# Attention with a bias on one core: the second half of pair 0's q is loaded after the bias's first half, and the four bias exps move one score slot back

## The chip, the core and the metric

The kernel runs on one core of a Trainium2 chip. The metric is the device time of one execution in microseconds. TensorE (PE), VectorE (DVE), ScalarE (ACT) and GpSimd (POOL) are engines that each take their own instructions in order; SyncE (SP) only issues DMAs here, and ScalarE and GpSimd issue some too.

## The reference

Four batches of eight heads, 1024 queries and 1024 keys of 64 numbers, one bias matrix shared by all heads:

```python
scale = 1.0 / np.sqrt(head_dim)
scores = scale * np.matmul(q, k.transpose(0, 1, 3, 2))
scores = scores + bias                       # bias: (1, 1, 1024, 1024)
scores_max = np.max(scores, axis=-1, keepdims=True)
attn = np.exp(scores - scores_max) / (np.sum(np.exp(scores - scores_max), axis=-1, keepdims=True) + 1e-8)
return np.matmul(attn, v).astype(np.float32)
```

## The kernel before

**The arithmetic.** The kernel uses exp(scale * s + b) = exp(scale * s) * exp(b) and subtracts no maximum. Scores are made transposed, keys on the partitions and queries along the row, so that the exps can go straight into the second matmul as its stationary operand. v carries a 65th column of ones, whose result is the row sum; a reciprocal and a multiply at the end divide by it.

**Pairs, banks and slots.** Two heads form a pair (`pr` 0 to 15), because two heads of 64 numbers fill the 128 partitions of one transpose. A *bank* is one score matmul: a head h of the pair, a query half qh (512 queries) and a key chunk kc (128 keys). There are 512 banks; in a pair the order is query half, key chunk, head, so that banks 0 to 15 are query half 0 of pair 0, banks 16 to 31 query half 1, and pair 1 starts at bank 32. Banks are gathered in *slots*: slot 0 is bank 0, slot 1 banks 1 and 2, and from slot 2 on each slot is three banks, `[3, 4, 5]`, `[6, 7, 8]` and so on. So slot 6 is banks 15, 16 and 17, the first that needs query half 1. A slot is one PSUM tile (`ps_s`, two buffers), filled by `s_fill` with three matmuls (line 130) and emptied by `s_exp` with one ScalarE instruction of 1536 elements (line 137), which writes the exps into the ring E (six tiles of 12 banks).

**The bias.** It is loaded in two halves of 1 MB (as bf16) into `btraw`. A *bias slot* `("B", qh, k0)` takes one of the two `ps_s` buffers: `b_fill` makes 16 transposes (line 145), and `b_exp` one ScalarE instruction of 2048 elements (line 150), which leaves exp(bias) for four key chunks of one query half in `eb`. There are four of them: (0, 0), (0, 4), (1, 0), (1, 4). VectorE multiplies E by `eb` (`mul_pair`, lines 156, 159, 162), which can start only when the first bias slot is through. The last two banks of the kernel, 510 and 511, get their bias on TensorE instead (`late_bias`, line 133).

**q and k.** Each pair's q and k are loaded as they are and transposed on TensorE in four pieces (`transpose_pe`, line 89): k or q, first or second half. A copy on VectorE takes a piece out of PSUM: for k line 102, for q line 98, which also multiplies by a mask so that each head's q has zeros where the other head's is. Pair 0 is loaded in parts: the first halves on SP's and ScalarE's queues (lines 244 to 247), the second half of k, the second half of q and the first half of the bias on GpSimd's queue, in this order:

```python
nc.gpsimd.dma_start(out=kr0[:, :, QC:, :]..., in_=kf[0][:, :, QC * D:])      # 261
nc.gpsimd.dma_start(out=qr0[:, :, QC:, :]..., in_=qf[0][:, :, QC * D:])      # 262
nc.gpsimd.dma_start(out=btraw[:, :QC, :], in_=bf_[:, :QC, :])                # 263
```

Behind them on this queue come v of pair 0, the bias's second half, and q, k and v of the next pairs (lines 317 to 321).

**The value matmuls.** `av_bank` adds one bank's share to the output of its unit (pair, head, query half) with four matmuls (line 187), in one of two PSUM buffers (`xa`, `xb`) that the transposed pieces use as well. When a unit's eight banks are in, VectorE divides (lines 197 and 199) and SP stores. The last unit is done by `av_last` in two halves of its queries (line 223), so that both can be finished side by side; its reciprocals are line 232.

**The order.** Slots 0 to 2 and the parts around them are written out by hand (lines 244 to 321). From slot 3 on a planner (lines 325 to 610) plays the three engines with given costs and due times and writes the instructions down in the order in which it starts them. ScalarE's order is fixed in the list `order`: the score slots in turn with the bias slots inserted. Before the change it begins S3, S4, S5, S6, B(0,0), S7, B(0,4), S8, S9, B(1,0), S10, B(1,4), S11. The due times `raw_at[0]` (the landing of pair 0's k and q second halves) and `bias_at` (the landing of the two bias halves) are in ns of the planner's clock; they cost no instruction, but decide where a step is put in TensorE's order. Since every engine works in order, a step that waits holds what is put behind it.

Of the kernel before, what the change touches and what calls it, by code (L numbers as in the profile page):

```python
# [15 lines left out]
def kernel(  # L16
# [15 lines left out]
    nc = tc.nc  # L32
# [7 lines left out]
    QC = NCH // 2  # L40
# [5 lines left out]
    bf_ = bias.rearrange("a b (p c) k -> p (a b c) k", p=P)  # L46
# [12 lines left out]
    btraw = consts.tile([P, NCH, S], BF)  # L59
# [47 lines left out]
    NB = len(banks)  # L107
# [106 lines left out]
    def av_last(x, bs, tag):  # L214
        first = len(last_left[x]) == 8
        if first:
            po[x] = (ps_x if tag != "s" else ps_s).tile([P, M, D1], F32, tag=tag, name="po")
        acc = po[x]
        for b in bs:
            last_left[x].remove(b)  # L220
        for i in range(M):
            for b in bs:
                nc.tensor.matmul(acc[:, i, :], e_at(b, 1)[:, 0, (x * M + i) * P:(x * M + i + 1) * P],
                                 vall[:, 2 * NP - 1, banks[b][3], :], start=first and i == 0 and b == bs[0],
                                 stop=not last_left[x] and b == bs[-1], skip_group_check=True)
        if last_left[x]:
            return None

        def evac():
            oh = small.tile([P, M, D], F32, name=f"oh{x}")  # L230
            rs = small.tile([P, M, 1], F32, name=f"rh{x}")
            nc.vector.reciprocal(rs[:], acc[:, :, D:D1])
            q = (nc.scalar, nc.sync)[x]
            if x == 0:
                for i in range(M):
                    nc.scalar.activation(oh[:, i, :], acc[:, i, :D], ACTF.Copy, scale=rs[:, i, :])
            else:
                nc.vector.tensor_tensor(oh[:], acc[:, :, :D], rs[:].to_broadcast([P, M, D]), op=ALU.mult)
            q.dma_start(out=of[2 * NP - 1][:, QC + x * M:QC + (x + 1) * M, :], in_=oh[:])
        return evac  # L240

    with tc.manual_schedule():
# [16 lines left out]
        nc.gpsimd.memset(qT0[D:, 0, :HQ], 0.0)  # L259
        nc.gpsimd.memset(qT0[:D, 1, :HQ], 0.0)  # L260
        nc.gpsimd.dma_start(out=kr0[:, :, QC:, :].rearrange("p t c d -> p t (c d)"), in_=kf[0][:, :, QC * D:])  # L261
        nc.gpsimd.dma_start(out=qr0[:, :, QC:, :].rearrange("p t c d -> p t (c d)"), in_=qf[0][:, :, QC * D:])
        nc.gpsimd.dma_start(out=btraw[:, :QC, :], in_=bf_[:, :QC, :])
        for x in range(2):
            for y in range(2):
                nc.vector.memset(mask[x * D:(x + 1) * D, y, :], 1.0 if x == y else 0.0)
# [59 lines left out]
        EXP, EXP0, QK, AV, TP = 427, 62, 216, 170, 350  # L326
        MUL, COPYQ, COPYK, EVAC, SEM = 600, 650, 420, 620, 80
        order = [("S", g) for g in range(3, NS)]
        for at, x in ((4, (0, 0)), (6, (0, 4)), (9, (1, 0)), (11, (1, 4))):
            order.insert(at, ("B",) + x)  # L330
        NO = len(order)
        T0 = 8000.0
# [2 lines left out]
        act_end = []  # L335
        x_free = {"xa": T0 - 500, "xb": T0 + 100}
        x_unit = {}
        bias_at = [13300, 20800]
        raw_at = {0: (5900, 7800), 1: (22200, 23500), 2: (26000, 28500)}
        pieces = [(0, 0, 1)]  # L340
        for pr in range(1, NP):
            pieces += [(pr, 1, 0), (pr, 0, 0), (pr, 1, 1), (pr, 0, 1)]
# [109 lines left out]
        def pe_last():  # L452

            best = None
            for x in range(2):
                left = last_left[x]
                if not left or (x == 1 and last_tag[0] is None):
                    continue
                steps = [[b] for b in left if b not in (NB - 4, NB - 3)] or [[NB - 4, NB - 3]]
                for bs in steps:  # L460
                    if any(b not in mul_at for b in bs):
                        continue
                    ready = max(mul_at[b] for b in bs) + SEM
                    tag = last_tag[x]
                    if tag is None and x == 0:
                        free, tag = min((x_free[y], y) for y in x_free)
                        ready = max(ready, free + SEM)
                    elif tag is None:
                        if len(act_end) < NO - 1 or len(filled) < NO:
                            continue  # L470
                        tag = "s"
                        ready = max(ready, act_end[NO - 2] + SEM)
                    c = (max(ready, t_pe), x, bs, tag)
                    if best is None or c[0] < best[0]:
                        best = c
            if best is None:
                return None
            ready, x, bs, tag = best
            cost = len(bs) * AV // 2

            def emit(t):
                if last_tag[x] is None and x == 0:
                    x_free[tag] = 1e12
                last_tag[x] = tag
                evac = av_last(x, bs, tag)
                if evac:
                    dve_q.append((t + cost + SEM, 1, EVAC, lambda t2: evac()))
            return ready, cost, emit

        def pe_av():  # L490
            if av_next >= NA:
                return pe_last()
            b = av_order[av_next]
            if b not in mul_at:
                return None
            ready = mul_at[b] + SEM
            u = unit_of(b)
            if banks[b][3] == 0:
                free, tag = min((x_free[x], x) for x in x_free)
                ready = max(ready, free + SEM)  # L500
            else:
                tag = x_unit[u]

            def emit(t):
                nonlocal av_next
                x_unit[u] = tag
                x_free[tag] = 1e12
                evac = av_bank(b, tag)
                av_next += 1
                if evac:  # L510
                    def run(t2):
                        evac()
                        x_free[tag] = t2 + EVAC
                    dve_q.append((t + AV + SEM, 3 if u == (NP - 1, 0, 1) else 1, EVAC, run))
            return ready, AV, emit
# [125 lines left out]
```

## Time and profile before

| | us |
|---|---|
| median of 7 runs | 250.39 (249.88 to 251.39) |
| the profiled execution | 250.58 |
| its span in the profile | 248.8 |
| ScalarE busy | 240.0 (96%) |
| TensorE busy | 229.3 (92%) |
| VectorE busy | 220.6 (89%) |
| first bias half: issue to landing | 9.4 |
| second bias half: issue to landing | 10.7 |

The span runs from the first to the last instruction of one execution; the time around it belongs to the execution too. Times in the timelines are us from the start of the span. A timeline line gives start, length, engine, line of the kernel, operation, what is written and read, the number of instructions merged into it, and in brackets how long the engine was idle before it and what ended that. The granted TensorE clock is 0.997 of full speed in the mean.

### The profile page before, as it was taken

To read this page: it belongs to the slowest core of one execution; us is meant where nothing else is said; L and a number is where in the kernel's file an instruction comes from. 1 tells how busy PE (TensorE), PEld (TensorE's weight loads), DVE (VectorE), ACT (ScalarE), POOL (GpSimd) and SP (SyncE) were. 2 spreads that over 40 slices of the span, in tenths; PEclk is the share of its full clock that TensorE was granted. 3 is DMA by queue.
4 is the path that set the end of the run, shared out by engine and by line. 5 is a ranking of instruction groups with operands and counts; after the bars stand their busy time and mean duration, and the time that the engine had idled before them with its cause. 6 is when DMAs were issued, how large, how long until landed. Compare 5 with 4: busy or idle time off the path is not lost.

```text
span 248.8 us, 7212 instructions
## 1 busy us (share of the span) xinstructions
PE 229.3 (92%) x3160; PEld 140.9 (57%) x3160; DVE 220.6 (89%) x393; ACT 240.0 (96%) x183; POOL 53.7 (22%) x74
## 2 busy tenths in 40 slices
PE   8768999999999999999999999999999999998991
PEld 4246656666555565655655665555565556565561
DVE  5236999999999999999999989999999999998882
ACT  5999999999999999999999999999999999999991
POOL 6653544104013050315050400501600000000000
PEclk9999999999999999999999999999999999999998
DMA  5999999924935659495868921592991101020211
GB/s 116 186 203 188 199 134 201 91 87 55 158 47 92 79 92 123 89 127 86 129 85 115 131 54 44 77 139 42 150 67 42 45 35 53 3 84 3 87 41 47
DMA packets 48464, 23.80 MB, mean 96 GB/s; under 512 B 34480, under 2 KB 44592, under 8 KB 48176
## 3 DMA queue, kind: packets, MB, share of 16 engines
q0 software_dynamic: 42272, 14.42, 53.5%
q1 hardware_dynamic: 5872, 8.72, 9.8%
q8 instruction: 25, 0.41, 0.7%
q10 hardware_dynamic: 288, 0.20, 0.2%
q14 instruction: 7, 0.06, 0.1%
HBM read 29.36 MB, written 8.39 MB: 152 GB/s over the span
## 4 chain that ended last, share of the span: by engine, by line
ACT 62%; PE 15%; DVE 14%; DMA 4%; issue 2%; POOL 1%; ACTq 0%; POOLq 0%
ACT E L137 59%; PE ps L130 10%; DVE E L162 5%; DMA btraw<-in_bias_dram 4%; PE po L187 3%; ACT eb L150 3%; DVE qT L98 2%; DVE E L159 2%; DVE oall L199 2%; PE px L89 1%; DVE E L156 1%; DVE rs L197 1%; DVE kT L102 1%; PE pb L145 0%; POOL kr L261 0%
## 5 line engine op out<-in xcount | busy, mean ns | idle before, releaser
L137 ACT ACTIVATE E<-ps 128x1536 bf16<-128x1536 f32 (+2 forms) x172 | 230.0, 1700 | 0.4 <-PE ps L130 0.4
L130 PE MATMUL ps<-qT,kT 128*128 128x512 bf16 x512 | 138.4, 378 | 8.2 <-ACT E L137 5.3
L187 PEld LDWEIGHTS <-E 128*128 128x128 bf16 x2016 | 81.4, 98 | 40.1 <-DVE E L162 5.2
L187 PE MATMUL po<-vall,E 128*128 128x65 bf16 x2016 | 92.6, 194 | 2.5 <-DVE E L162 1.3
L159 DVE TENSOR_TENSOR E<-E,eb 128x2048 bf16<-128x2048 bf16 x66 | 79.8, 1217 | 6.9 <-ACT eb L150 6.5
L162 DVE TENSOR_TENSOR E<-E,eb 128x1024 bf16<-128x1024 bf16 x116 | 76.7, 684 | 2.7 <-ACT E L137 1.9
L130 PEld LDWEIGHTS <-kT 128*128 128x128 bf16 x512 | 45.1, 96 | 39.5 <-issue 8.4
L75 POOL DMA_DIRECT2D kr<-in_k_dram x15 | 10.5, 701 | 90.4 <-PE px L89 84.5
L81 POOL DMA_DIRECT2D vall<-in_v_dram x32 | 28.2, 885 | 4.6 <-DVE kT L315 3.6
L199 DVE TENSOR_TENSOR oall<-po,rs 128x256 f32<-128x256 f32 x63 | 26.7, 425 | 2.2
L98 DVE TENSOR_TENSOR qT<-px,mask 128x1024 bf16<-128x1024 bf16 x31 | 21.3, 688 | 3.9 <-PE px L89 3.1
L76 POOL DMA_DIRECT2D qr<-in_q_dram x15 | 10.8, 718 | 30.0 <-PE px L89 25.5
L102 DVE COPY kT<-px 128x512 bf16<-128x512 bf16 x30 | 12.6, 421 | 1.8 <-PE px L89 1.2
L197 DVE RECIPROCAL rs<-po 128x4 f32<-128x4 f32 x63 | 11.2, 177 | 2.0 <-PE po L187 1.7
L89 PEld LDWEIGHTS <-qr 128*64 128x64 bf16 x248 | 8.0, 109 | 8.6 <-issue 5.9
L89 PE MATMUL px<-ident,qr 128*64 128x128 bf16 x248 | 12.8, 225 | 0.0
L89 PE MATMUL px<-ident,kr 128*64 128x128 bf16 x240 | 12.4, 224 | 0.1
L89 PEld LDWEIGHTS <-kr 128*64 128x64 bf16 x240 | 7.7, 109 | 7.8 <-issue 3.6
L150 ACT ACTIVATE eb<-pb 128x2048 bf16<-128x2048 bf16 x4 | 7.5, 1879 | 0.4 <-PE pb L145 0.4
L145 PE MATMUL pb<-ident,btraw 128*128 128x128 bf16 x64 | 4.7, 226 | 2.5 <-ACT eb L150 1.5
L145 PEld LDWEIGHTS <-btraw 128*128 128x128 bf16 x64 | 4.4, 147 | 3.3 <-issue 1.6
L156 DVE TENSOR_TENSOR E<-E,eb 128x1024 bf16<-128x1024 bf16 (+2 forms) x7 | 4.6, 686 | 0.2 <-ACT E L137 0.2
(44 smaller groups left out, 27.2 us busy)
## 6 DMA issues: line engine op xcount, KB each, us to landing
out_dram<-oall SPq DMA_DIRECT2D x28, 256.0 KB, 2.0
vall<-in_v_dram POOLq DMA_DIRECT2D x32, 128.0 KB, 6.2
kr<-in_k_dram POOLq DMA_DIRECT2D x15, 256.0 KB, 4.2
qr<-in_q_dram POOLq DMA_DIRECT2D x15, 256.0 KB, 5.8
btraw<-in_bias_dram POOLq DMA_DIRECT2D x2, 1024.0 KB, 10.0
out_dram<-oall SPq DMA_DIRECT2D x7, 128.0 KB, 3.8
k0f<-in_k_dram SPq DMA_DIRECT2D x2, 128.0 KB, 3.0
q0f<-in_q_dram ACTq DMA_DIRECT2D x1, 128.0 KB, 2.7
```

The source lines that it names most:

```text
L81: nc.gpsimd.dma_start(out=vall[:, 2 * pr + t, :, :D], in_=vf[pr, :, t])
L89: nc.tensor.transpose(px[t * D:(t + 1) * D, c, :], src[:, t, half * QC + c, :], ident[:])
L98: nc.vector.tensor_tensor(dst[:, :, half * HQ:(half + 1) * HQ], px.rearrange("p c q -> p (c q)").unsqueeze(1).to_broadcast([P, 2, HQ]), ma ...
L102: nc.vector.tensor_copy(dst[:, half * QC:(half + 1) * QC, :], px[:])
L130: nc.tensor.matmul(ps[:, j, :], kT[:, kc, :], qT[:, h, qh * HQ:(qh + 1) * HQ], start=True, stop=b not in late_bias)
L137: nc.scalar.activation(e_at(slots[g][0], n), open_ps.pop(("S", g))[:, :n, :], ACTF.Exp, scale=scale)
L150: nc.scalar.activation(eb[:, qh, k0:k0 + 4, :], open_ps.pop(("B", qh, k0))[:, :4, :], ACTF.Exp)
L159: nc.vector.tensor_tensor(e, e, eb[:, qh, kc:kc + 2, :].unsqueeze(2).to_broadcast([P, 2, 2, HQ]), op=ALU.mult)
L162: nc.vector.tensor_tensor(e, e, eb[:, qh, kc:kc + 1, :].to_broadcast([P, n, HQ]), op=ALU.mult)
L187: nc.tensor.matmul(acc[:, i, :], e[:, 0, i * P:(i + 1) * P], vall[:, 2 * pr + h, kc, :], start=(kc == 0 and i == 0), stop=(kc == NCH - 1), ...
L197: nc.vector.reciprocal(rs[:], acc[:, :, D:D1])
L199: nc.vector.tensor_tensor(oall[:, c0:c0 + QC, :], acc[:, :, :D], rs[:].to_broadcast([P, QC, D]), op=ALU.mult)
```

## The change

Three things. On GpSimd's queue the load of the second half of pair 0's q is issued after the load of the bias's first half instead of before it. The four bias slots are inserted one place later in `order`, which then begins S3, S4, S5, S6, S7, B(0,0), S8, B(0,4), S9, S10, B(1,0), S11, B(1,4), S12; the planner's due times for the landings are set to match. And in the plan of the last unit, banks 508 and 509 (`NB - 4`, `NB - 3`) are steps of their own, each as soon as it is multiplied, instead of one step of two banks behind all others.

```diff
@@ -259,8 +259,8 @@
         nc.gpsimd.dma_start(out=kr0[:, :, QC:, :].rearrange("p t c d -> p t (c d)"), in_=kf[0][:, :, QC * D:])
+        nc.gpsimd.dma_start(out=btraw[:, :QC, :], in_=bf_[:, :QC, :])
         nc.gpsimd.dma_start(out=qr0[:, :, QC:, :].rearrange("p t c d -> p t (c d)"), in_=qf[0][:, :, QC * D:])
-        nc.gpsimd.dma_start(out=btraw[:, :QC, :], in_=bf_[:, :QC, :])
@@ -326,7 +326,7 @@
         order = [("S", g) for g in range(3, NS)]
-        for at, x in ((4, (0, 0)), (6, (0, 4)), (9, (1, 0)), (11, (1, 4))):
+        for at, x in ((5, (0, 0)), (7, (0, 4)), (10, (1, 0)), (12, (1, 4))):
             order.insert(at, ("B",) + x)
@@ -335,8 +335,8 @@
-        bias_at = [13300, 20800]
-        raw_at = {0: (5900, 7800), 1: (22200, 23500), 2: (26000, 28500)}
+        bias_at = [12900, 20200]
+        raw_at = {0: (5900, 13700), 1: (22200, 23500), 2: (26000, 28500)}
@@ -456,7 +456,7 @@
-                steps = [[b] for b in left if b not in (NB - 4, NB - 3)] or [[NB - 4, NB - 3]]
+                steps = [[b] for b in left]
                 for bs in steps:
```

## The prediction

> **What bounds the kernel now.** I read the page's busy times first, then ScalarE's timeline, then the chain of waits, then TensorE's and VectorE's timelines around the four bias slots, and last the DMA landings and GpSimd's issues. The busy times say that ScalarE (ACT) is the long engine:
>
> ```profile
> PE 229.3 (92%) x3160; PEld 140.9 (57%) x3160; DVE 220.6 (89%) x393; ACT 240.0 (96%) x183; POOL 53.7 (22%) x74
> ```
>
> ScalarE's timeline (start, length, line, count, and in brackets the idle time before) says where the missing 4% is:
>
> ```profile
> 5.60 1.57 ACT L137 ACTIVATE E<-ps 128x512 bf16<-128x512 f32 x2 [0.18 <-PE ps L130]
> 7.38 6.82 ACT L137 ACTIVATE E<-ps 128x1536 bf16<-128x1536 f32 x5 [0.20 <-PE ps L130]
> 14.62 1.88 ACT L150 ACTIVATE eb<-pb 128x2048 bf16<-128x2048 bf16 x1 [0.42 <-PE pb L145]
> 16.39 1.44 ACT L137 ACTIVATE E<-ps 128x1536 bf16<-128x1536 f32 x1
> ...
> 27.15 215.97 ACT L137 ACTIVATE E<-ps 128x1536 bf16<-128x1536 f32 x161
> ```
>
> From 7.38 us to 243.12 us ScalarE has one wait, 0.42 us before the first bias exp. After it the exps follow each other at 215.97 / 161 = 1.341 us. An exp without a wait begins about 0.11 us before its predecessor's listed end (16.39 against 14.62 + 1.88 = 16.50), so that wait costs 0.42 + 0.11 = 0.53 us. Everything after 14.62 is a gapless run of fixed length: whatever delays ScalarE before it moves the end by as much, and a later engine can't give it back.
>
> Who holds ScalarE at 14.62 is told by the chain of waits and by the first landings:
>
> ```profile
> 3.26 0.71 POOL qr L262
> 3.97 9.36 DMA btraw<-in_bias_dram
> 13.33 0.05 issue
> 13.37 1.22 PE pb L145 x16
> 14.62 1.88 ACT eb L150
> ```
>
> ```profile
> kr<-in_k_dram POOLq DMA_DIRECT2D x1, 128.0 KB, 3.5
> qr<-in_q_dram POOLq DMA_DIRECT2D x1, 128.0 KB, 5.0
> ```
>
> GpSimd issues k's second half at 2.43, q's at 3.26 and the bias at 3.97; they land at 2.43 + 3.5 = 5.9, 3.26 + 5.0 = 8.3 and 3.97 + 9.36 = 13.33. On TensorE and VectorE, the same stretch:
>
> ```profile
> 8.14 0.39 PE L130 MATMUL ps<-qT,kT 128*128 128x512 bf16 x1 [0.33 <-DVE kT L315]
> 8.88 0.81 PE L130 MATMUL ps<-qT,kT 128*128 128x512 bf16 x3 [0.35 <-ACT E L137]
> 9.62 0.41 PE L89 MATMUL px<-ident,qr 128*64 128x128 bf16 x8
> 10.22 0.81 PE L130 MATMUL ps<-qT,kT 128*128 128x512 bf16 x3 [0.19 <-ACT E L137]
> 11.56 0.81 PE L130 MATMUL ps<-qT,kT 128*128 128x512 bf16 x3 [0.54 <-ACT E L137]
> ```
>
> ```profile
> 10.07 0.69 DVE L98 TENSOR_TENSOR qT<-px,mask 128x1024 bf16<-128x1024 bf16 x1 [1.99 <-PE px L89]
> 16.53 2.36 DVE L159 TENSOR_TENSOR E<-E,eb 128x2048 bf16<-128x2048 bf16 x2 [5.76 <-ACT eb L150]
> ```
>
> The second half of q is transposed at 9.62, copied at 10.07, and first used at 11.56: that is score slot 6, banks 15, 16 and 17, of which 16 and 17 are query half 1. Its exp is the last of the five at 7.38, ends at 14.20 and began near 14.20 - 1.44 = 12.76.
>
> **Moved: the q load behind the bias.** GpSimd's two issues swap; their sum (0.72 + 0.58 = 1.30 us) and what follows in that queue are unchanged, and SP's and ACT's queues are not passed. The three landings came in the order of issue, and all three are issued by 4.56 in either order, so I take the queue as served in order: the same bytes end at the same time, only the last arrival is now q's. Hence q's second half lands at 13.33 instead of 8.3. Low end: some engines run dry of the bias early; at 1024 KB in 13.33 - 8.26 = 5.07 us, q's 128 KB are 0.63 us, so 12.7. High end: v's first pieces, issued from 8.13 on, share the engines, and GpSimd's wait for one of them ends only at 14.75: 14.7. The diff's own due time is 13.7. I take 13.33, the row of the same bytes.
>
> From there the chain to ScalarE is, in this trace's durations: start of the transposes 0.04 (13.33 to 13.37 for the bias), eight transposes 0.41, hand-over 0.04, VectorE's masked copy 0.69, hand-over 0.05 (8.14 after kT's copy), the two matmuls of banks 16 and 17: (0.81 - 0.38) / 2 + 0.38 = 0.59, hand-over 0.04. Bank 15 doesn't need it; the row at 8.14 shows one bank waiting alone for its half while the others were already filled. Sum 1.86, so slot 6's exp begins at 15.19 instead of 12.76: **2.43 us later**. This lies wholly on the path: slots 3 to 5 are the only exps whose data is there, they end near 12.86, and ScalarE takes its instructions in order, so slot 7 and the bias exp stand behind the wait.
>
> **Moved: the four bias slots.** The bias's first half now lands before 13.33, its transposes need the score buffer that slot 6's exp frees near 16.63, take 1.21 us, and lie under slot 7's 1.34. The 0.53 us wait is thus gone: **-0.53 us**. Cover of the other three is the same single score exp (1.34 against 1.13 to 1.21 plus 0.09 of hand-overs), the second bias half is used 3 us later than now; taken at nothing, with 0.1 us each if a queued value matmul stands in front, so 0 to 0.4 in all. Slot 11, which needs pair 1, is filled near 25.6, about as now (25.84), from transposes that now start at 22.29 and 23.64: nothing.
>
> VectorE's first multiply goes from 16.53 to the first bias exp's new end: slot 6 from 15.19 to 16.64, slot 7 to 17.98, bias to 19.75, so 3.2 us later, where ScalarE is 1.9 later. The extra 1.3 us of backlog must fit into idle time. The stretches from 27.15 to 243 show VectorE idle for 9.8 us in sum (0.6 to 1.3 in each 25), so it is absorbed; if it isn't, up to 1.3 us come at the end. I take 0. The E ring holds 72 banks; 21 instead of 18 wait at its fullest start.
>
> **Changed: the last value steps.** Banks 508 and 509 become single steps instead of a pair. The number of matmuls is the same. Four of them, 0.92 / 20 = 0.05 us each, can run before bank 509's multiply. What stands behind is VectorE, busy with the other unit's division until 243.81 and at the last reciprocals from 243.75:
>
> ```profile
> 242.98 0.92 PE L223 MATMUL po<-vall,E 128*128 128x65 bf16 x20 [0.19 <-DVE E L156]
> ```
>
> So -0.2 to +0.2, taken 0. The due times at lines 338 and 339 cost no instruction; they make the plan put q's transposes after slot 5's fill instead of after slot 4's.
>
> **Sum.** 2.43 - 0.53 = +1.90 us. The profiled execution took 250.58 (span 248.8 and 1.8 around it), so 252.48; the median of the seven runs is 0.19 lower: **252.3**.
>
> **Rival 1, TensorE loses its clock too.** Slot 5's fill ends at 11.03; with slot 6 blocked TensorE idles until 13.37, 2.34 us. The longest idle time after the start is now 1.32 us, and the granted clock stays 1.00. If the clock fell, the rate is that of the first dummies, 12 of 256 columns in 2.74 us, 0.11 us for 128 columns: eight transposes +0.5, two score matmuls +0.4, and 16 bias transposes 1.8 instead of 1.2 behind slot 7's cover, +0.5: 0.9 to 1.4 more, **253.5**. The unabsorbed backlog ends there as well. The Trainium skill (TensorE: Matmul & The Clock Gate, Part 1, What's actually happening) has the array fall to half rate after an idle window of about 3.4 us; by that rule 2.34 us alone does not reach it and the sum stays as it is, while no row of this trace shows an idle time of this length.
>
> **Rival 2, faster: q is not held up by the bias.** If its packets were served beside the bias's, q would land near 3.84 + 5.0 = 8.8, slot 6 would keep its place, and only the -0.53 us would remain: **249.9**. The break-even landing follows from the sum: 13.33 - 1.90 = 11.43. Against it: the landings in order of issue, and 1024 KB that took 5 us between q's landing and their own; q would have to overtake 40% of it.
>
> **Rival 3, no change.** q lands near 11.4 by partial sharing, or ScalarE's delay is taken back later. The second is excluded by the 161 gapless exps; the first needs the same overtaking.
>
> **How the numbers follow.** In-order service with the rows' durations: 0.82. Rival 1 (clock or backlog on top): 0.11. Rival 2: 0.04. Rival 3: 0.03. The bounds of q's landing alone, 12.7 to 14.7, give 251.7 to 253.7; the tail's 0.2 lowers the lower end to 251.6, and rival 1's middle lies inside. Less than 2 in 10 lies outside. A run of this kernel tells about 0.3% (0.75 us) from no change; +0.75 needs a landing after 12.2, below my low end, so nearly the whole of the first two cases is slower.
>
> **What would show it.** ScalarE's timeline: three exps from slot 3 on, then an idle time of about 2.3 us released by TensorE's L130, slot 6 at 15.2, and no wait before any L150. TensorE: L89 on qr at 13.4 with a wait for the DMA of qr; the first L145 near 16.7. VectorE: L98 near 13.8, the first L159 near 19.8. Then 161 exps or so without a gap at 1.341, and the same 5.7 us behind the last one. I am wrong if L89 starts before 12, if ScalarE has a wait later on, or if the stretch after slot 6 is not the length of before.

## The result and the profile after

The changed kernel is slower. Its median is 254.19 us over 23 runs (251.30 to 255.21) where the kernel before has 250.67 over 60 (249.69 to 253.54); the ratio is 1.011, with an interval of 1.009 to 1.0129. The two numbers differ because its times lie in two groups with a gap between them, so a median falls into one group and the ratio weighs both. The ratios leave out executions that took over 1.5% longer than the fastest of their kernel: one here, one of the loads alone and four of the version with the bias slots moved the other way, both further down. On the 250.39 us that the prediction started from, the ratio gives 253.1 us, inside the range; the median of 254.19 lies 0.5 us above the range's upper end.

The profile that came with it is of a short execution: 251.74 us, span 250.0. ScalarE's timeline, as in the prediction:

```profile
8.19 5.48 ACT L137 ACTIVATE E<-ps 128x1536 bf16<-128x1536 f32 x4 [0.20 <-PE ps L130]
14.11 2.79 ACT L137 ACTIVATE E<-ps 128x1536 bf16<-128x1536 f32 x2 [0.44 <-PE ps L130]
16.80 1.88 ACT L150 ACTIVATE eb<-pb 128x2048 bf16<-128x2048 bf16 x1
...
24.95 1.88 ACT L150 ACTIVATE eb<-pb 128x2048 bf16<-128x2048 bf16 x1 [0.47 <-PE pb L145]
...
29.84 214.61 ACT L137 ACTIVATE E<-ps 128x1536 bf16<-128x1536 f32 x160
```

The run of four ends with slot 5 at 13.67. Then ScalarE waits for slot 6, released by TensorE's line 130. The first bias exp at 16.80 follows slot 7 without a wait. The third one waits 0.47 us, which is new. From 29.84 on 160 exps follow each other at 214.61 / 160 = 1.341 us, as before. TensorE in front of slot 6, and the landing it waits for:

```profile
11.04 0.81 PE L130 MATMUL ps<-qT,kT 128*128 128x512 bf16 x3 [0.53 <-ACT E L137]
12.28 0.41 PE L89 MATMUL px<-ident,qr 128*64 128x128 bf16 x8 [0.44 <-DMA qr<-in_q_dram]
12.63 0.39 PE L130 MATMUL ps<-qT,kT 128*128 128x512 bf16 x1
13.48 1.24 PE L130 MATMUL ps<-qT,kT 128*128 128x512 bf16 x5 [0.47 <-DVE qT L98]
```

```profile
qr<-in_q_dram POOLq DMA_DIRECT2D x1, 128.0 KB, 8.4
```

Slot 5's fill, then a wait for the DMA of q, the eight transposes, bank 15 alone at 12.63, and at 13.48 banks 16 and 17 of slot 6 with slot 7's three. q was issued at 3.82 and landed 8.4 us later, at 12.2; the kernel before had it at 8.3. VectorE follows:

```profile
12.74 0.69 DVE L98 TENSOR_TENSOR qT<-px,mask 128x1024 bf16<-128x1024 bf16 x1 [3.84 <-PE px L89]
18.70 2.36 DVE L159 TENSOR_TENSOR E<-E,eb 128x2048 bf16<-128x2048 bf16 x2 [5.27 <-ACT eb L150]
```

In this execution slot 6 starts 1.35 us later than before (14.11 against 12.76), and the span is 1.2 us longer. That the two numbers are close is chance: behind slot 6 the old wait of 0.53 us before the first bias exp is gone, the third bias exp costs about as much anew, and the end is 0.1 us shorter. Most executions lost more, and the experiments had to say why.

### The profile page after: what moved, and what is told of

Its sections match the earlier page's. It is cut to its first block, busy times and chain, and to the rows that moved or that the text cites. A ratio compares the mean times of both kernels' runs of the same rounds, so it can differ in the third digit from the quotient of the medians.

```text
span 250.0 us, 7212 instructions
## 1 busy us (share of the span) xinstructions
PE 229.9 (92%) x3160; PEld 141.3 (57%) x3160; DVE 220.2 (88%) x392; ACT 240.0 (96%) x183; POOL 53.7 (21%) x74
## 4 chain that ended last, share of the span: by engine, by line
ACT 64%; DVE 14%; PE 10%; DMA 5%; issue 3%; POOL 1%; ACTq 0%
ACT E L137 62%; PE ps L130 6%; DVE E L162 4%; DMA kr<-in_k_dram 4%; DVE E L159 4%; PE po L187 2%; DVE oall L199 2%; DVE qT L98 2%; ACT eb L150 1%; DMA q0f<-in_q_dram 1%; DVE E L156 1%; PE px L89 1%; POOL vall L81 1%; DVE rs L197 1%; DVE kT L102 1%
## 5 line engine op out<-in xcount | busy, mean ns | idle before, releaser
L159 DVE TENSOR_TENSOR E<-E,eb 128x2048 bf16<-128x2048 bf16 x67 | 80.8, 1216 | 5.5 <-ACT eb L150 5.3
L162 DVE TENSOR_TENSOR E<-E,eb 128x1024 bf16<-128x1024 bf16 x114 | 75.5, 684 | 2.7 <-ACT E L137 1.9
```

The lines of the kernel that those rows point to most:

```text
L159: nc.vector.tensor_tensor(e, e, eb[:, qh, kc:kc + 2, :].unsqueeze(2).to_broadcast([P, 2, 2, HQ]), op=ALU.mult)
L162: nc.vector.tensor_tensor(e, e, eb[:, qh, kc:kc + 1, :].to_broadcast([P, n, HQ]), op=ALU.mult)
```

## The experiments

The first theory was the prediction's: q lands behind the bias and slot 6 waits for it. The executions above 253 us had a granted clock of 0.98 to 0.991 where the shorter ones had 0.990 to 0.998, so the half clock of the prediction's rival 1 was the second suspect, and a landing that varies by itself the third.

**The same kernel again, four times.** No edit.

> The changed kernel once more, for the spread of its times and the granted clock of each run. Theory A (q's load and TensorE's clock): two groups of times, near 251.7 us with a clock of 0.994 to 0.998 and near 254.3 us with 0.98 to 0.991; a profile of the second group has a stretch at half clock of one or two times 3.4 us, after slot 5, in which bias transposes and score matmuls take twice as long and ScalarE waits for them. Theory B (the landing of q varies by itself): the profile of a long run has q landing 2 us or more later than in a short one, and the waits lie in front of slot 6 only.

> The changed kernel, one more profile. Theory A2: the time follows the landing of q: near 12.3 us it takes 251.3 to 252.4 us, near 14.2 us with a half-clock stretch on TensorE 253.5 to 255. A long execution with an early landing would speak for the clock alone.

> The changed kernel, another profile, with the same expectations: landing near 12.3 us and 251.3 to 252.4 us, or near 14.2 us with a half-clock stretch and 253.5 to 255 us.

> The changed kernel once more, on the same chip and beside the same runs as the three that follow. Theory A2: times from 251.2 to 255 us; those above 253 us with a granted clock of 0.992 or less.

Measured: ratios 1.0071 (1.004 to 1.0103) and 1.0126 (1.0077 to 1.0174) in the two timed sets. Over all 44 executions whose clock is on record, 18 took 251.2 to 252.9 us at a clock of 0.990 to 0.998, and 26 took 253.4 to 255.2 us at 0.980 to 0.991; none lies between. (The kernel before is not free of a lower clock: of its 87 executions beside these versions, nine had 0.992 or less, and they took 251.2 to 252.7 us.) The first of these profiles is a long one, 254.93 us. Its line of ScalarE, its two of TensorE and its landing:

```profile
16.71 2.79 ACT L137 ACTIVATE E<-ps 128x1536 bf16<-128x1536 f32 x2 [3.93 <-PE ps L130]
```

```profile
14.24 0.64 PE L89 MATMUL px<-ident,qr 128*64 128x128 bf16 x8 [3.29 <-DMA qr<-in_q_dram]
...
15.66 2.16 PE L130 MATMUL ps<-qT,kT 128*128 128x512 bf16 x5 [0.25 <-DVE qT L98]
```

```profile
qr<-in_q_dram POOLq DMA_DIRECT2D x1, 128.0 KB, 10.4
```

q needs 10.4 us instead of 8.4, and then the transposes take 0.64 us instead of 0.41 and the five matmuls 2.16 instead of 1.24: TensorE works at half clock. Both theories hold at once. The other three profiles separate them. With a landing after 8.4 us and a full clock slot 6 starts at 14.14 (251.22 us). With a landing after 8.5 us and a half clock it starts at 14.65 (251.95 us), so the expectation that an early landing goes with a full clock was wrong. With a landing after 8.9 us and a half clock that comes a little later it starts at 14.57, and the first bias exp waits 0.61 us more (252.70 us).

What brings the half clock is seen in the stretches of 3.4 us (us, busy time and count of PE, PEld, DVE, ACT and POOL, granted clock, DMA share, GB/s). First the execution of 254.93 us, then those of 251.95 and 251.22:

```profile
10.70:14.10 3.40, 0.25 (x2) 0.00 (x0) 0.00 (x0) 2.08 (x2) 2.08 (x4) 1.00 1.64 174
14.10:17.50 3.40, 3.02 (x14) 1.24 (x15) 0.69 (x1) 0.79 (x1) 2.68 (x4) 0.50 1.22 225
```

```profile
9.90:13.30 3.40, 1.54 (x12) 0.56 (x12) 0.45 (x1) 3.38 (x3) 3.40 (x6) 1.00 1.77 166
13.30:16.70 3.40, 2.84 (x11) 1.26 (x11) 0.25 (x1) 2.05 (x2) 2.90 (x4) 0.50 1.02 178
```

```profile
9.70:13.10 3.40, 1.54 (x12) 0.56 (x12) 0.33 (x1) 3.11 (x3) 3.40 (x6) 1.00 1.67 171
```

Here the half clock lasts one stretch of 3.4 us and stands behind a stretch in which TensorE was busy for 0.25 of 3.40 us (7%) in the first and 1.54 (45%) in the second. In the second the longest idle time was 0.94 us, less than the 1.32 us that the kernel before has without harm. The third execution had the same 45% in nearly the same place, even with a longer gap (1.33 us), and kept its clock. So the longest gap doesn't decide. A low busy share stands ahead of every half clock that was seen, but 45% went both ways, so what else decides, perhaps where a stretch begins, is not shown.

**The three parts alone.** The first has the loads swapped and the due times of the change, the second only the later bias slots, the third only the single last steps.

```diff
 # loads only
+nc.gpsimd.dma_start(out=btraw[:, :QC, :], in_=bf_[:, :QC, :])
 nc.gpsimd.dma_start(out=qr0[:, :, QC:, :]..., in_=qf[0][:, :, QC * D:])
-nc.gpsimd.dma_start(out=btraw[:, :QC, :], in_=bf_[:, :QC, :])
-bias_at = [13300, 20800];  raw_at = {0: (5900, 7800), ...
+bias_at = [12900, 20200];  raw_at = {0: (5900, 13700), ...
 # order only
-for at, x in ((4, (0, 0)), (6, (0, 4)), (9, (1, 0)), (11, (1, 4))):
+for at, x in ((5, (0, 0)), (7, (0, 4)), (10, (1, 0)), (12, (1, 4))):
 # steps only
-steps = [[b] for b in left if b not in (NB - 4, NB - 3)] or [[NB - 4, NB - 3]]
+steps = [[b] for b in left]
```

> The two loads swapped, with the due times of the change; the bias slots and the last steps as before. Theory A: slot 6 still waits for q and TensorE still runs dry before it, so about the time of the changed kernel, 253 to 254.5 us as a median, with the same two groups; without the wait before the third bias exp perhaps 0.5 us less. If the later bias slots are what costs, it is near the kernel before, 250 to 251 us.

> Only the bias slots one place later; loads and due times as before. Theory A: q is there at 8.3, slot 7's exp fills the time in which the bias is awaited, so the wait of 0.42 us before the first bias exp goes; 249.9 to 250.4 us, and the clock stays at 0.996 or more. If the later bias slots cost by themselves (the backlog of VectorE and TensorE, or a wait before the third bias exp), 250.9 us or more.

> Only the last value steps: banks 508 and 509 as steps of their own. All theories: within 0.2 us of the kernel before, the stretch from the last exp's end to the end of the span 5.6 to 5.7 us. It would be a cost of its own if that stretch grew by 0.3 us or more.

Measured: the loads alone 253.54 us, ratio 1.0089 (1.0053 to 1.0126), again in two groups (250.6 to 251.7 and 253.5 to 254.9). The order alone 250.48 us, ratio 1.0006 (0.9979 to 1.0033). The steps alone 250.66 us, ratio 1.001 (0.9986 to 1.0033), and 5.7 us from the last exp's end to the end of the span, as in the kernel before. So the loss comes with the swapped loads. Their due times were not run apart from them; the rows show TensorE waiting for the DMA of q itself.

The order alone did not gain the half microsecond that it was expected to, and its clock was 0.991 to 1.0 where 0.996 or more was expected. Its profile is of its longest execution (253.00 us) and shows the first bias exp without a wait, but then, on ScalarE and on TensorE:

```profile
24.52 1.88 ACT L150 ACTIVATE eb<-pb 128x2048 bf16<-128x2048 bf16 x1 [1.52 <-PE pb L145]
```

```profile
22.95 0.41 PE L89 MATMUL px<-ident,kr 128*64 128x128 bf16 x8 [1.78 <-DMA kr<-in_k_dram]
23.30 1.19 PE L145 MATMUL pb<-ident,btraw 128*128 128x128 bf16 x16
```

The third bias slot, one place later, now stands behind pair 1's k transposes in TensorE's order, and these wait for a load that lands near 22.9 here. From 24.7 on TensorE is then at half clock for 3.4 us, and ScalarE waits another 0.76 and 0.40 us. The 0.47 us in the changed kernel's profile go back to the same load: k lands at 21.50 there, and VectorE's copy of it and the multiply behind the copy hold TensorE. How often it comes can't be told from one profile of each.

The half microsecond is not there to be had in every execution either. In the profile of the steps alone, whose bias slots stand as in the kernel before, slot 2 began at 9.14, and the first bias exp follows slot 6 without a wait:

```profile
9.14 6.82 ACT L137 ACTIVATE E<-ps 128x1536 bf16<-128x1536 f32 x5 [1.15 <-PE ps L130]
15.86 1.88 ACT L150 ACTIVATE eb<-pb 128x2048 bf16<-128x2048 bf16 x1
```

**TensorE kept busy.** The changed kernel with 14 matmuls on zeros in front of q's transposes, whose results nothing reads.

```diff
 def emit(t):
     pieces.pop(0)
+    if pr == 0:
+        dm = ps_x.tile([P, HQ // 2], F32, tag=tag, name="dm")
+        for _ in range(14):
+            nc.tensor.matmul(dm[:], zeros[:, :P], zeros[:], start=True, stop=True)
     copy = transpose_pe(pr, which, half, tag) if pr < NP else late_bias_pe(tag)
```

> The changed kernel with 14 matmuls on zeros (256 columns each, 1.5 us) added on TensorE between slot 5's fill and q's transposes; nothing else moves in any engine's order. Theory A2 (the long executions are q's late landing, near 14.2 us, plus 0.65 us from the half clock that TensorE's idle time brings): the granted clock stays at 0.994 or more in all runs; executions in which q lands late take about 253.6 us instead of 254.2, those in which it lands early lose up to 1.1 us to the zeros, about 252.5; so the two groups move together and the highest time falls below 254. Theory C (the clock is the main part of the 2.5 us between the groups): no time above 252.5 us. Theory B (the landing alone): clocks or not, the highest times stay at 254.2 to 255.

> The 14 matmuls on zeros again, now beside the changed kernel on one chip. Theory A2 (late landing and, on top of it, the half clock): the granted clock is 0.994 or more in every run and nothing lies above 253.7 us; the highest times are 0.6 to 1.5 us below the highest of the changed kernel. If the landing alone makes the high times, they stay where they are.

Measured: 252.02 us (250.76 to 253.00), ratio 1.0065 (1.0042 to 1.0089), and beside the changed kernel on one chip 252.14 us (251.09 to 253.67), ratio 1.0055 (1.0032 to 1.0079) against 1.0126. In all 24 executions the clock is 0.993 or more, and the group above 253.7 us is gone. The second of its profiles has a late landing (10.2 us) and a full clock; TensorE and ScalarE:

```profile
11.19 1.69 PE L436 MATMUL dm<-zeros 128*128 128x256 bf16 x14
14.09 0.41 PE L89 MATMUL px<-ident,qr 128*64 128x128 bf16 x8 [1.21 <-DMA qr<-in_q_dram]
```

```profile
15.92 2.79 ACT L137 ACTIVATE E<-ps 128x1536 bf16<-128x1536 f32 x2 [2.74 <-PE ps L130]
```

From the first transpose to slot 6's exp it is 15.92 - 14.09 = 1.83 us here, and 16.71 - 14.24 = 2.47 in the long execution: the half clock costs 0.64 us in front of slot 6. What stays is the landing, a wait of 2.74 us. The theory that the clock is the main part expected nothing above 252.5 us and fell. The theory of the landing alone expected 254.2 us and more, but the times don't settle it: both profiles with the zeros have 4.7 us from the last exp to the end of the span, where the profiles of the changed kernel have 5.5 to 6.6, so some 0.8 us or more of the lower times may have come from the end and not from the clock. Against it stand the rows, with 0.64 us less in front of slot 6 behind an equally late landing. The profile with an early landing (8.6 us) took 251.31 us, where 252.5 was expected.

**Less of the bias ahead of q.** The first half of the bias is split into two DMAs, with q after two rows of four, or after three.

```diff
-nc.gpsimd.dma_start(out=btraw[:, :QC, :], in_=bf_[:, :QC, :])
+nc.gpsimd.dma_start(out=btraw[:, :QC // 2, :], in_=bf_[:, :QC // 2, :])     # or QC - 1
 nc.gpsimd.dma_start(out=qr0[:, :, QC:, :]..., in_=qf[0][:, :, QC * D:])
+nc.gpsimd.dma_start(out=btraw[:, QC // 2:QC, :], in_=bf_[:, QC // 2:QC, :])
-bias_at = [12900, ...   raw_at = {0: (5900, 13700), ...
+bias_at = [13300, ...   raw_at = {0: (5900, 11500), ...                      # or 12600
```

> The changed kernel with q's second half behind half of the bias's first half only (two rows of four, then q, then the other two rows); due times 13.3 for the bias and 11.5 for q. Theory A2: q lands near 10.8 us, before the break-even of 11.4, so slot 6 keeps its place and the bias is covered by slot 7; no second group, 250.2 to 250.9 us, as with the loads left alone. If being behind any of the bias costs, or the extra DMA does, 251.5 us or more.

> The changed kernel with q's second half behind three of the four rows of the bias's first half, the fourth behind q; due times 13.3 for the bias and 12.6 for q. Theory A2: the cost grows with the landing of q and only beyond 11.4 us. q lands near 11 us in a quick execution and near 12.5 in a slow one: 250.3 to 252 us, between the version with half of the bias ahead (250.5) and the changed kernel. If it is the split into two DMAs that freed the version with half, this one is as fast as that.

Measured: with half ahead 250.47 us, ratio 1.0005 (0.9986 to 1.0024); with three quarters 251.29 us, ratio 1.0033 (1.0009 to 1.0057). q landed 6.2 us after its issue with half ahead, and 9.0 us with three quarters. That is no sooner than the 8.4 to 8.9 us of the changed kernel's early landings, so these profiles don't show that the landing follows the dose, and two executions of the second version (252.64 and 253.26 us) lay above the 252 that was expected. Both versions have the split, and only the one with three quarters ahead is clear of the kernel before, so the split alone is unlikely to be what helps. With half ahead ScalarE has no wait left behind slot 2:

```profile
7.91 8.20 ACT L137 ACTIVATE E<-ps 128x1536 bf16<-128x1536 f32 x6 [0.33 <-PE ps L130]
16.01 1.88 ACT L150 ACTIVATE eb<-pb 128x2048 bf16<-128x2048 bf16 x1
...
28.48 214.65 ACT L137 ACTIVATE E<-ps 128x1536 bf16<-128x1536 f32 x160
```

From slot 2's start to the last exp's end it is 28.48 + 214.65 - 7.91 = 235.22 us, where the kernel before has 27.15 + 215.97 - 7.38 = 235.74. This doesn't show that the later bias slots are worth the 0.5 us that the prediction gave them: in this profile slot 2 itself began 0.53 us later and the whole half of the bias had landed by 12.5 us, so the wait would be covered in the old order too. The steps alone, with the old order, have the same 28.41 + 215.95 - 9.14 = 235.22. The start of slot 2 lies between 7.25 and 9.14 us over the 14 profiles.

**The bias slots moved the other way.** The loads as changed, but B(0,0) before slot 6.

```diff
-for at, x in ((5, (0, 0)), (7, (0, 4)), (10, (1, 0)), (12, (1, 4))):
+for at, x in ((3, (0, 0)), (5, (0, 4)), (9, (1, 0)), (11, (1, 4))):
```

> The changed kernel with the bias slots moved the other way: B(0,0) stands before slot 6 and B(0,4) before slot 7, the last two where the kernel before has them. Theory A2: with the bias landing at 11.3 to 13.2 us, its exp of 1.77 us stands where slot 6 waited, and q's transposes and copy (1.9 us after its landing at 12.3 to 14.2) lie under it; ScalarE waits 0 to 0.9 us before B(0,0) and at most 0.3 before slot 6; 250 to 251 us and no group above 252. If the order of the loads costs whatever stands in the slots, 252 us or more.

Measured: 252.12 us, from 249.37 to 254.09 us, ratio 1.0011 (0.9974 to 1.0048). Over all twelve executions the mean is 251.90 us, against 250.77 of the kernel before beside it. The expectation of no group above 252 us was wrong. Its profile is one of the long ones (253.71 us), on TensorE and ScalarE:

```profile
13.39 1.92 PE L145 MATMUL pb<-ident,btraw 128*128 128x128 bf16 x16 [2.07 <-DMA btraw<-in_bias_dram]
```

```profile
15.35 1.88 ACT L150 ACTIVATE eb<-pb 128x2048 bf16<-128x2048 bf16 x1 [2.20 <-PE pb L145]
```

The bias landed 10.1 us after its issue, TensorE ran dry just the same, and the 16 transposes took 1.92 us at half clock instead of 1.21. This order trades the wait for q for a wait for the bias; its shortest execution, 249.37 us, and its longest are both far from the middle. None of the versions is faster than the kernel before beyond the intervals.

## Why the prediction was right, and where it was not

**The number: right in part by luck.** The sum of 252.3 us was made for one landing. The executions fall into two groups, 18 from 251.2 to 252.9 us and 26 from 253.4 us on, and 253.1 is a weighing of the two that lies in the gap where none of the 44 executions was. Two of the prediction's own signs of being wrong came true in the short profile: a wait later on (0.47 us), and a stretch after slot 6 that is not the length of before.

**Slot 6 waits for q, and nobody gives it back: right.** The wait is where it was forecast, released by line 130, and the exps behind it keep 1.341 us. The parts alone put the loss on the swapped loads.

**The chain from the landing to slot 6: right to the hundredth.** 1.82 us were summed from the first transpose to the exp; 14.11 - 12.28 = 1.83 at full clock, and 1.83 with the zeros in front.

**The wait before the first bias exp: gone, its worth not shown.** It is gone where the clock is full. With the order alone slot 2 began at 7.25, earlier than in the kernel before, and the first bias exp at 15.33 follows slot 7 without a wait; there the later slot does what was forecast. That it gives 0.53 us to the end is not shown by any time: the order alone is no faster, and the profile of the steps alone lacks the wait with the old order.

**The landing: order right, size wrong.** In all nine profiles of versions with the whole half ahead of q, q lands 0.6 to 0.8 us behind the bias. The Trainium skill (DMA: Bandwidth & Descriptors, Two DMAs through the same engine are not ordered) says that descriptors of one queue and engine start in order, and that nothing orders DMAs across the engines; the order of the landings here agrees with the first. But the same bytes did not take the same time: q came at 12.2 to 12.7 us in six of the nine and at 14.0 to 14.2 in three, where 13.33 was taken and 12.7 was the low end. Since slot 6 waits for an absolute time, it also hides a late start: slot 2 began 0.81 us later in the short profile, and that cost nothing.

**The third bias slot: inside its 0 to 0.4 us and a little over.** 0.47 us of waiting in one profile of five; its cause, the load of pair 1's k, was not among the prediction's reasons.

**The clock: the step that failed.** Rival 1 got a chance of 0.11 because 2.34 us of idle time seemed too short. All 26 long executions had a lowered clock (0.991 or less), and of the five profiles of the changed kernel three have a stretch at half clock here; two of these three are short executions (251.95 and 252.70 us), so the half clock alone doesn't make a long one. Its price was near the forecast where it was measured (0.64 us of the 0.9 given to the transposes and fills; 0.61 us before the first bias exp in the execution of 252.70, where 0.5 was given). The reason was wrong: the Trainium skill (TensorE: Matmul & The Clock Gate, Part 1, What's actually happening) speaks of an idle window of about 3.4 us, and the prediction read it as one gap of that length. Here gaps of 0.94 us or less in a stretch that was 45% busy were enough in one execution, and not in another.

**The tail: the edit cost nothing, but the end moved.** The single last steps changed nothing that can be measured. The time from the last exp to the span's end, which the prediction held at 5.7 us, was 4.7 to 6.6 us over the profiles; the last stores took 3.5 us to land in the execution of 254.93 us, and 1.6 in the one of 252.31, against 2.6 before. No run ties this to the change.

With these sizes the prediction's own sum meets both ends. Short: 252.48, less 1.08 for slot 6 (14.11 instead of 15.19), plus 0.58 for the third bias slot (0.47 and the usual overlap of 0.11) where before 0.09 was lost, less 0.15 in the tail: 251.74, and 251.74 was measured. Long: 252.48, plus 1.52 for slot 6 (0.87 of landing and 0.64 of clock), plus 0.94 in the tail: 254.94, and 254.93 was measured. These sums are made after the fact, from the profiles that they explain.

**What stays open.** Why the same loads land up to 2 us apart was not found. Only one profile of the changed kernel fell into the group above 253 us, so that a late landing goes with all of them is an inference from that one, from the late landings of two other versions (14.0 us each) and from the gap that the nine landings leave between 12.7 and 14.0.

## What to carry to other kernels

When the bounding engine has no gaps, a load that is moved behind a larger one costs its new landing time less the time at which its first user is due, in full; write the break-even landing down first. If the load has to move, splitting the larger one so that the small one goes ahead of its second half cost nothing here (250.47 us), and gained nothing either. A wait that empties TensorE has a second price, since the engine that comes out of it may run at half clock: look at what TensorE does in the 3.4 us ahead (7% to 51% busy before every half clock seen here), not only at its longest gap. Where an order stands behind a load whose landing varies, look at several executions, since one profile shows one landing.

## What the hardware showed that was not expected

- TensorE went to half clock for 3.4 us (once for twice that, with B(0,0) before slot 6) after stretches of 3.4 us in which it was busy for 0.25, 1.49, 1.50, 1.54 and 1.75 us (7% to 51%); the longest single gap in one of them was 0.94 us. Another stretch of 45%, with a gap of 1.33 us, left the clock at full.
- The bias's first half, 1024 KB behind the same 128 KB, landed 8.3 to 10.2 us after its issue in different executions of one program.
- The last 64 KB stores took 1.6 to 3.6 us to land.
